# Copies of V and of bias tables in DRAM paced one by one by TensorE, half of V's made earlier, and 12 filler steps instead of 8 ahead of the second attention half

## The chip, the cores and the metric

The kernel runs on one core of one Trainium2 chip. The metric is the device time of one execution in microseconds (us), lower is better; where several executions are measured, their median is taken. The core has a matrix engine (TensorE, PE in the profile), VectorE (DVE), ScalarE (ACT) and GpSimd (POOL), and a queue that issues nearly all transfers in this kernel, SyncE (SP, or SPq for its queue). The engines work through their own instruction streams in order and wait for each other by semaphores.

## The reference

One layer of an encoder on x (1 x 2048 x 1024, float32). After a layer norm with modulation, one input projection (1024 to 9216 columns) feeds two branches: a bidirectional gated linear recurrence (8 heads of 128) and a neighbourhood attention on a grid of 32 rows x 64 columns (16 heads of 64). One output projection, the gated residual and a last layer norm follow. Cut to what bears on the change:

```
def _hgrn2_branch(q_in, i_in, zf_fw, zf_bw, g_in, lb_fw, lb_bw, norm_g):
    ...
    o = direction(zf_fw, lb_fw, False) + direction(zf_bw, lb_bw, True)
    o = _rmsnorm(o.transpose(0, 2, 1, 3), norm_g).reshape(B, S, HG_WIDTH)
    return o.astype(g_in.dtype) * jax.nn.silu(g_in)

def _neighbourhood_attention(q, k, v, rpb):
    """2-D neighbourhood attention. ...
    Each query (r, col) attends to the KR x NA_KC window clamped inside the grid.
```

The attention adds a bias from the table rpb to each score; a query sees 8 rows x 16 columns.

## The kernel before

The sequence is worked on in two halves of 1024 tokens, and the work of TensorE is written out in its final order, a main stream woven with a dense stream of projections. The order of SyncE's, ScalarE's and VectorE's instructions is set by a scheduler with its own estimate of time, except for instructions marked `pinned`, which keep the order of the program among themselves.

The stages are: startup; the first attention half (8 head pairs) up to about 545 us of the trace; the recurrence, 16 units (8 heads by two sequence halves) of `hgrn`, woven with the projections of the unit to come, up to about 1745; the second attention half, 8 head pairs; and the rest of the output projection, up to 2632.

*Weights.* `dma` loads a piece of weights into `wr` (L251, L790), ScalarE copies it to `wh` (L257) and VectorE takes the rest `wl` (L258), so that a float32 product is made of three faster matmuls (L267, L280 for V). Four `wr` buffers go round.

*V.* `vproj` (L280, evacuated as `vt` at L286) writes V of a group of two head pairs to a DRAM tensor `nv_d[p2]` (L288), p2 = 0 to 3, both halves of the sequence. The second attention half reads V column window by column window. `window(p2, j)` (L1360) copies for one of four column offsets j all 32 grid rows, 32 columns each, from `nv_d[p2]` to `nw_d[p2]`, 1 MB from DRAM to DRAM, so that the loads at L978 (`V<-nw`, or `q<-nw` where the buffer's name is that of q) are simple ones. The source rows of the first sequence half are written in the first attention half, those of the second half only near the border.

*The border.* The last unit of the recurrence is woven with `border_dense`: V's projection for p2 = 0, the projections for the first head pair of the second half, V's projection for p2 = 1. Behind dense steps 7, 15, 23 and 31 it calls `window(0, j)`. The unit's own tail (`hgrn_tail`) loads tiles `cl` from DRAM: `cl<-qb` (L666), `cl<-op` (L667), `cl<-sgd` (L668); TensorE multiplies (L671), VectorE adds (L672), and the norm follows: `t` (ScalarE, L331), `rh` (VectorE, L333), sums on TensorE (L339, L340), and a store `yq<-t` (L347). L344 is the product of that norm which reads the `cl` tile for the last time.

*The second attention half.* Before it, K of the first pair is copied by ScalarE into `KA` and `KB` (L970), each on one half of the partitions, and a DMA mirrors it to the other half (L971); Q (L954, L955) and the gate `sg` (L990) are made. TensorE starts with 8 filler steps of V's projection for p2 = 2 and 3 (`vs`; a step is 24 matmuls at L280), then come the scores of the first pair (L1038, L1042). The other filler steps are woven into the first pair. In the pairs u = 0 to 2, `window(u + 1, j)` is called at the task steps 1, 2, 3 and 4.

*Tables.* `expand()` writes the bias tables of the second half in DRAM, as a side stream of the recurrence that is advanced once per group (two groups per unit): first one DMA that fills the parts of `ebot_d` outside the grid with a large negative number (L747, 64 x 24 rows of 256 numbers, all read from one source row; called the fill here), then 24 steps (8 pairs x 3) of three table copies (L744). All are `pinned`. A second side stream, `wo_prepare`, splits the output weights (L414 to L420: `bk`, `wod`). `op`, `qb` and `sgd` (L653 to L659) are the recurrence's own stores.

Of the kernel before, what the change touches and what calls it, by code (L numbers as in the profile page):

```python
# [19 lines left out]
P = 128  # L20
KT = D // P
HALF = 1024
GRP = 512
NHEAD = 8
NPAIR = 8
GW = 64
# [6 lines left out]
KS = (0, 8, 24, 32)  # L33
# [4 lines left out]
def body(ctx: ExitStack, tc: tile.TileContext, t):  # L38
    nc = tc.nc
    dve, act, pool, pe = nc.vector, nc.scalar, nc.gpsimd, nc.tensor  # L40
    dma = nc.sync.dma_start
# [22 lines left out]
    def dram(name, shape, dt=F32):  # L64
        if name in t:
            return t[name]
        return nc.dram_tensor(name, shape, dt, kind="Internal").ap()
# [11 lines left out]
    nv_d = [dram(f"nv{i}", (SEQ, 256)) for i in range(4)]  # L79
    nw_d = [dram(f"nw{i}", (4, SEQ // 2, 256)) for i in range(4)]  # L80
# [49 lines left out]

    def pinned(ins):
        return tc.keep_in_program_order(ins)

    def mod_init():
        mod["c"] = tl("cb", shape=[P, D])
        cs = [cp.tile([P, KT], F32, name=f"cs{i}") for i in range(2)]
        dma(cs[0], t["c"])
        act.activation(cs[1], cs[0], AF.Exp, scale=-1.0)
        sigmoid(cs[1])
        dve.tensor_mul(cs[1], cs[0], cs[1])  # L140
        act.dma_start(c_d.rearrange("(p k) -> p k", k=KT), cs[1])
        act.dma_start(mod["c"], c_d.rearrange("(o n) -> o n", o=1).to_broadcast([P, D]))
        dve.tensor_scalar(adab1, adab[:, 8:16], 1.0, 1.0, op0=ALU.mult, op1=ALU.add)
# [264 lines left out]
    aside = []  # L408
# [13 lines left out]
    def hgrn(u, half, st, tail):  # L422
# [8 lines left out]
        def rates(d, g):  # L431
            col = d * 8 + u
            e = zs[d, g]
            dve.tensor_scalar_min(e, e, ECAP)
            L = tl("g")
            act.activation(L, e, AF.Ln, bias=1.0)
            c = tl("c")
            act.activation(c, e, AF.Ln, scale=lbt[:, col:col + 1], bias=1.0)
            r = tl("g")
            act.activation(r, L, AF.Exp, scale=-1.0, bias=l1m[:, col:col + 1])  # L440
            dve.tensor_tensor(e, e, r, op=ALU.mult)
            for b in range(4):
                lo, hi = b * P, (b + 1) * P
                if d == 0:
                    sl = slice(lo, hi)
                else:
                    sl = slice(hi - 1, lo - 1 if lo else None, -1)
                dve.tensor_tensor_scan(c[:, sl], c[:, sl], L[:, sl], 0.0, op0=ALU.add, op1=ALU.subtract)
            return c, e
# [20 lines left out]
        def turned(src, tag):  # L470
            pk = ps("tr")
            for b in range(4):
                pe.transpose(pk[:, b * P:(b + 1) * P], src[:, b * P:(b + 1) * P], ident)  # L473
            ke = tl(tag)
            act.activation(ke, pk, AF.Copy)
            return ke
# [100 lines left out]
        for g in range(2):  # L577
            v = turned(vts[g], "v")
            next(tail, None)
            cs, ks = {}, {}  # L580
            cs[0], ks[0] = rates(0, g)
            yield 5
            next(tail, None)
            cs[1], ks[1] = rates(1, g)
            de0 = ends(0, g, cs[0], ks[0])
            yield 5
            next(tail, None)
            ke0 = turned(de0, "ke")
            de1 = ends(1, g, cs[1], ks[1])
            kx, qx = diagonal_factors(g, cs, ks)  # L590
            yield 3
            next(tail, None)
            forward_states(g, updates(ke0, v))
            ke1 = turned(de1, "ke")
            yield 3
            next(tail, None)
            pu = updates(ke1, v)
            if g == 0:
                ub = tl("ub")
                act.activation(ub, pu, AF.Copy)  # L600
                ubs[g] = ub
            else:
                ubs[g] = pu
            pb = diagonal(kx, qx)
            lf = [(w, *level_factors(w, g, cs, ks)) for w in (32, 64)]
            yield 6
            next(tail, None)
            pa = ps("pa")
            for w, xk, xq in lf:
                level(w, pa, xk, xq)  # L610
            pm = masked(pa, pb)
            yield 5
            outputs(g, v, pm)
            for z in aside:
                next(z, None)
# [120 lines left out]
    def flat(tab, offset, *dims):  # L736
        return bass.AP(tab.tensor, offset, [list(d) for d in dims])

    def expand():

        def put(dst, row, off, width, tab, jt, nrow, row0, nq, n):
            src = tab[jt, 0, row0, 0, 0:1]
            to = dst[row, off:off + 1]
            pinned(dma(flat(to, to.offset, (width, 16), (16 * width, nq), (1, n * 64)), flat(src, src.offset, (nrow * 64, 16), (64, nq), (1, n * 64))))  # L744

        to, big = ebot_d[0, 0, 0, 0:1], tint[0, 0, 0, 0, 0, 0:1]
        pinned(dma(flat(to, to.offset, (768, 64), (P * 768, NPAIR * 3), (1, 256)), flat(big, big.offset, (0, 64), (0, NPAIR * 3), (1, 256))))  # L747
        for p in range(NPAIR):
            for jt in range(3):
                put(emid_d[p, jt], 0, 0, 960, tint[p], jt, 22, 0, 8, 15)  # L750
                put(ebot_d[p, jt], 0, 256, 768, tedge[p], jt, 15, 0, 4, 8)
                put(ebot_d[p, jt], 64, 0, 768, tint[p], jt, 22, 4, 4, 12)
                yield
# [157 lines left out]
    NLEN = 2 * len(NCOL) * KT * KUS  # L911
    VLEN = 8 * 2.9
# [442 lines left out]
            st = nxt  # L1355
        return r

    def window(p2, j):
        src, to = nv_d[p2][KS[j], 0:1], nw_d[p2][j, 0, 0:1]
        dma(flat(to, to.offset, (32 * 256, 32), (1, 32 * 256)), flat(src, src.offset, (GW * 256, 32), (1, 32 * 256)))  # L1360

    def border_dense(dense):
        yield from vstream(0)
        for i, s in enumerate(dense):
            yield s
            if i % 8 == 7 and i < 32:
                window(0, i // 8)
        yield from vstream(1)

    BTOT = NLEN + 2 * VLEN  # L1370
# [48 lines left out]
    with psum_phase("h", *HPS), phase("h", HB, SMH), tc.manual_schedule(engines={mybir.EngineType.PE}):  # L1419
# [4 lines left out]
        for i in range(16):  # L1424
            half, u = divmod(i, 8)
            if i < 15:
                nxt = hgrn_dense((i + 1) % 8, (i + 1) // 8, i in (6, 7), reload if i == 6 else None)
                tail, st = weave(hgrn(u, half, st, tail), nxt, HTOT, HSUM, lead=20 * KUS if i == 0 else 0.0)
            else:
                raws, dense = natten_stream(0, 1)  # L1430
# [139 lines left out]
    with psum_phase("n1", *NPS), phase("n1", NB1, SM1), tc.manual_schedule(engines={mybir.EngineType.PE}):  # L1570
        natten_init(6, 1)
        st = st0
        for f, *a in ((st.k, 0), (st.k, 1), (st.k, 2), (st.q, 1), (st.table, "mid", 0), (st.table, "mid", 1), (st.table, "mid", 3), (st.v, 0), (st.v, 1), (st.v, 2), (st.v, 3), (st.q, 2), (st.v, 4), (st.gate, 1)):
            f(*a)
        def border_values():
            for i, s in enumerate(vstream(2, 3)):
                yield s
                if i == 13:
                    feed.split(1)

        vs = border_values()
        for _ in range(8):
            next(vs)
        pipe = []
        cts = [(c + u * P) // P for u in range(1, 8) for _ in range(2 if u == 7 else 1) for n, c in NCOL]
        feed = Feed(cts)
        feed.at = 0
        for u in range(8):
            nxt, extra = None, {j + 1: [(window, u + 1, j)] for j in range(4)} if u < 3 else None
            if u < 7:  # L1590
                raws, dense = natten_stream(u + 1, 1, feed, u + 1 == 7)
                total = NLEN
                if u == 0:
                    dense, total = chain(vs, dense), NLEN + VLEN
                nxt = Prep(u + 1, 1, raws)
                if u == 6:
                    extra = {6: [(wo_get, 0, 0)], 7: [(wo_get, 0, 1)], 9: [(wo_get, 0, 2)], 10: [(wo_get, 0, 3), (y_split, 0)], 11: [(wo_get, 0, 4, 5), (y_early, 2)]}
                    for i in (2, 3):
                        extra[i] = [(lambda tt: y_early(tt, alloc=lambda: tl("wr")), i - 2)]
            else:  # L1600
                y_split(1)
                dense, total = out_stream(list(range(NE))), NE * 16 * KUS
                wo_get(0, 6, 7)
                y_early(3)
                extra = {1: [(wo_get, 1, 0, 1)], 2: [(wo_get, 1, 2)], 3: [(wo_get, 1, 3, 4)], 4: [(wo_get, 1, 5)], 5: [(wo_get, 1, 6, 7)]}
            weave(natten_woven(st, nxt, pipe, extra), dense, total, 24)
            st = nxt
        sums(pipe, 2)
        turn(pipe, 2)
        turn(pipe, 1)  # L1610
        sums(pipe, 0)
# [70 lines left out]
```

## Time and profile before

| what | value |
|---|---|
| runs before | 2630.04 us median of 3 (2628.11 to 2630.34) |
| profiled execution | 2633.74 us |
| its span | 2632.0 us, mean granted clock 0.994 |
| matmuls (L267, L280 and all others) | 17328 |
| copies nw<-nv | 16, 1024 KB each |
| table copies emid<-tint, ebot<-tedge, ebot<-tint | 24 each, and the fill |

The profile shows one execution, with times from the start of the span. A wait row reads: engine, waiting tile and line, the releaser, then total us, number of waits, longest. A row of the chain of waits reads: start, duration, what ran or was under way, each step released by the one above; a DMA in it runs from its issue to its landing. A timeline row has start, duration, engine, line, operation, output<-input, shape, and in brackets the idle time of the engine before it with what ended it. A row of windows has the stretch, its length, the busy time with the number of instructions, TensorE's granted clock (1.00 is full speed), the DMA engines' share and GB/s. Lines are those of the kernel before.

### The profile page before, as it was taken

The numbers are of one execution on the slowest core, as the hardware profiler recorded it, in microseconds if no ns is written. First come the engines' busy times: TensorE is split into PE (matmuls) and PEld (weight loads), VectorE is DVE, ScalarE is ACT, GpSimd is POOL, SyncE is SP. The second block draws the span as 40 slices with busy tenths as digits, with TensorE's granted clock in tenths as the row PEclk, the third lists the DMA queues.
The fourth block names the chain that finished last, engine by engine and source line by source line (L and its number), as shares of the span: only waits on it lengthen the run. The fifth ranks groups of instructions, "written<-read, shape, count | busy, mean of one in ns | idle before, by whom it ended". The sixth has DMA issues, their size and how long they took to land.

```text
span 2632.0 us, 45961 instructions
## 1 busy us (share of the span) xinstructions
PE 2570.7 (98%) x17328; PEld 2150.6 (82%) x17328; DVE 1756.1 (67%) x4351; ACT 1417.5 (54%) x2808; POOL 97.9 (4%) x119
## 2 busy tenths in 40 slices
PE   5999999999999999999999999989999999999998
PEld 3888888878888888888888888788888888788887
DVE  6446445478777778877778777546778888658443
ACT  4434445376666666666667666345666666531110
POOL 0000000000000000000000000000000000032221
PEclk9999999999999999999999999999999999999999
DMA  7555454243233337333221222567444445643331
GB/s 261 170 171 156 135 184 138 98 99 135 96 103 114 106 124 261 129 107 98 95 84 57 73 73 81 165 203 255 130 136 135 136 147 181 200 148 128 97 96 56
DMA packets 246061, 352.83 MB, mean 134 GB/s; under 512 B 31575, under 2 KB 121943, under 8 KB 245207
## 3 DMA queue, kind: packets, MB, share of 16 engines
q1 hardware_dynamic: 245551, 349.37, 41.5%
q8 instruction: 136, 2.23, 0.3%
q14 instruction: 86, 0.70, 0.1%
q10 hardware_dynamic: 288, 0.53, 0.1%
HBM read 266.21 MB, written 113.39 MB: 144 GB/s over the span
## 4 chain that ended last, share of the span: by engine, by line
PE 89%; DMA 4%; DVE 4%; ACT 2%; issue 1%; SPq 0%; DVEq 0%; ACTq 0%
PE pj L267 49%; PE pj L280 6%; PE ps L1499 4%; PE ps L1498 4%; PE ps L1500 4%; PE ps L1106 4%; PE ps L1087 3%; PE ps L481 2%; PE ps L1038 2%; PE ps L473 1%; PE ps L1042 1%; PE ps L548 1%; DMA nw<-nv 1%; PE ps L572 1%; PE ps L574 1%; PE ps L520 1%
## 5 line engine op out<-in xcount | busy, mean ns | idle before, releaser
L267 PE MATMUL pj<-h,wh 128*128 128x512 f32 x4016 | 1278.7, 399 | 9.0 <-ACT h L232 5.9
L267 PEld LDWEIGHTS pj<-h,wh 128*128 128x128 f32 x4016 | 731.5, 188 | 165.7 <-issue 13.4
L267 PE MATMUL pj<-h,wl 128*128 128x512 f32 x2008 | 787.3, 392 | 0.0
L267 PEld LDWEIGHTS pj<-h,wl 128*128 128x128 f32 x2008 | 377.4, 188 | 82.5
L1060 ACT ACTIVATE pbuf<-pbuf,mx 128x480 f32<-128x480 f32 (+2 forms) x224 | 143.0, 639 | 143.1 <-DVE mx L1055 142.2
L280 PE MATMUL pj<-wh,h 128*128 128x256 f32 x1024 | 193.2, 287 | 0.9 <-ACT wh L826 0.7
L1055 DVE CUSTOM_DVE_ANT_1 pbuf<-ps,bias 128x480 f32<-128x480 f32 (+2 forms) x224 | 125.8, 590 | 101.1 <-PE ps L1042 85.8
L258 DVE TENSOR_TENSOR wl<-wr,wh 128x512 fp32r<-128x512 f32 x192 | 131.5, 685 | 53.8 <-ACT wh L257 53.0
L280 PEld LDWEIGHTS pj<-wh,h 128*128 128x128 f32 x1024 | 162.3, 192 | 4.7 <-issue 1.9
L257 ACT ACTIVATE wh<-wr 128x512 fp32r<-128x512 f32 x192 | 120.0, 625 | 68.3 <-PE pj L267 55.9
L280 PE MATMUL pj<-wl,h 128*128 128x256 f32 x512 | 145.2, 284 | 0.4 <-DVE wl L827 0.4
L1093 ACT ACTIVATE pt<-ps 128x512 f32<-128x512 f32 (+1 forms) x128 | 68.9, 538 | 85.9 <-PE ps L1087 84.2
L1091 DVE COPY pt<-ps 128x512 f32<-128x512 f32 (+1 forms) x128 | 79.0, 619 | 49.6 <-PE ps L1087 48.9
L774 ACT ACTIVATE e<-pj 128x512 f32<-128x512 f32 x100 | 59.1, 592 | 89.0 <-PE pj L267 83.5
L1471 ACT ACTIVATE yh<-yr 128x512 fp32r<-128x512 f32 x52 | 32.7, 629 | 134.6 <-PE ps L1499 115.7
L1087 PE MATMUL ps<-ident,pbuf 128*128 128x128 f32 x776 | 103.3, 273 | 0.0
L1087 PEld LDWEIGHTS ps<-ident,pbuf 128*128 128x128 f32 x776 | 90.8, 141 | 13.6 <-issue 0.2
L1554 DVE TENSOR_TENSOR vt<-ps,gt 128x512 f32<-128x512 f32 x24 | 16.5, 692 | 128.1 <-PE ps L1500 128.1
L827 DVE TENSOR_TENSOR wl<-wr,wh 128x512 fp32r<-128x512 f32 x68 | 46.8, 690 | 80.8 <-ACT wh L826 76.6
L280 PEld LDWEIGHTS pj<-wl,h 128*128 128x128 f32 x512 | 98.5, 192 | 1.3 <-DVE wl L827 0.6
L1065 DVE TENSOR_SCALAR pbuf<-pbuf,mx 128x480 f32<-128x480 f32 (+2 forms) x224 | 96.0, 437 | 5.4
L1106 PE MATMUL ps<-pt,V 128*64 128x128 f32 x1408 | 96.7, 277 | 0.8 <-DMA V<-nv 0.8
(278 smaller groups left out, 4694.3 us busy)
## 6 DMA issues: line engine op xcount, KB each, us to landing
wr<-in_w_in SPq DMA_DIRECT2D x276, 256.0 KB
nw<-nv SPq DMA_DIRECT2D x16, 1024.0 KB
yr<-yq SPq DMA_DIRECT2D x60, 256.0 KB
emid<-tint SPq DMA_DIRECT2D x24, 480.0 KB
bias<-emid SPq DMA_DIRECT2D x24, 480.0 KB
V<-nw SPq DMA_DIRECT2D x40, 256.0 KB
bias<-ebot SPq DMA_DIRECT2D x24, 384.0 KB
x<-in_x SPq DMA_DIRECT2D x32, 256.0 KB
```

The costliest lines, as they stand in the source:

```text
L257: act.activation(hi, raw, AF.Copy)
L258: dve.tensor_tensor(lo, raw, hi, op=ALU.subtract)
L267: pe.matmul(pz, a, b, start=(k == 0 and n == 0), stop=(k == KT - 1 and n == 2))
L280: pe.matmul(pzs[tp][:, i * 256:(i + 1) * 256], a, b, start=(k == 0 and n == 0 and i == 0), stop=(k == KT - 1 and n == 2), skip_group_check ...
L1055: return dve.tensor_tensor_reduce(s[:, 0:nk].rearrange("p (r c) -> p r c", c=32), sc[:, 0:nk].rearrange("p (r c) -> p r c", c=32), bt[:, 0 ...
L1060: act.activation(s[:, 0:nk], s[:, 0:nk], AF.Exp, scale=-1.0, bias=mx[:, 0:1], accum_out=mx[:, 1:2])
L1065: dve.tensor_scalar(s[:, 0:nk], s[:, 0:nk], mx[:, 2:3], 1.0, op0=ALU.mult, op1=ALU.mult)
L1087: pe.transpose(ptp[:, c * P:(c + 1) * P], s[:, c * P:(c + 1) * P], ident)
L1106: pe.matmul(self.po[R][hs_, j * P:(j + 1) * P], self.st.V[c0 + c][:, j * P + hh * 64:j * P + hh * 64 + 64], pts[hh][:, c * P:(c + 1) * P], ...
L1498: pe.matmul(pz, yh[:, kk], wh, start=first, stop=False)
L1499: pe.matmul(pz, yh[:, kk], wl, start=False, stop=False)
L1500: pe.matmul(pz, yl[:, kk], wh, start=False, stop=last)
```

## The change

- `paced(ins)` is new: it makes a DMA wait for the TensorE instruction that was emitted last before it in the program. The fill, the table copies and the V copies use it; the first two were `pinned`, the V copies had neither.
- `window` has a third argument, the sequence half, and copies 16 grid rows, 512 KB, so that there are 32 copies.
- The copies of half 0 go into `expand()`: four steps, one for each j, ahead of the tables of pairs 0, 2, 4 and 6. `expand()` begins with 8 empty steps and is advanced once more per group, in the middle of it. It had 24 steps with copies and now has 8 empty ones and 40 with copies; both end with unit 11.
- The copies of half 1 stay where the whole ones were, further apart: for p2 = 0 behind dense steps 5, 17, 29 and 41 of the border, for the others at task steps 3, 5, 7 and 9 of the pairs u = 0 to 2.
- 12 filler steps instead of 8 come ahead of the first scores of the second half; four are left for the first pair, whose `total` is smaller accordingly.

The number of matmuls and their operands stay. Lines in the changed kernel are higher: by 5 up to the new `next(aside[1], None)`, by 16 in the second attention half; `window` is at L747, the fill at L759, the table copies at L756.

```
+    def paced(ins):
+        mm = next(i for i in reversed(nc.cur_bb.bb.instructions) if i.engine == mybir.EngineType.PE)
+        tc.add_manual_dep(ins.ins, mm.name, mybir.DependencyInfo(mybir.DependencyClass.Sync, mybir.DependencyReason.DATA), reason="paced")
+        return ins
...
             yield 3
+            next(aside[1], None)
             next(tail, None)
             pu = updates(ke1, v)
...
+    def window(p2, j, half):
+        src, to = nv_d[p2][half * HALF + KS[j], 0:1], nw_d[p2][j, half * (HALF // 2), 0:1]
+        paced(dma(flat(to, to.offset, (32 * 256, 16), (1, 32 * 256)), flat(src, src.offset, (GW * 256, 16), (1, 32 * 256))))
+
     def expand():
+        for _ in range(8):
+            yield
...
         for p in range(NPAIR):
+            if p % 2 == 0:
+                for j in range(4):
+                    window(p // 2, j, 0)
+                    yield
...
         for i, s in enumerate(dense):
             yield s
-            if i % 8 == 7 and i < 32:
-                window(0, i // 8)
+            if i % 12 == 5:
+                window(0, i // 12, 1)
...
         vs = border_values()
-        for _ in range(8):
+        for _ in range(12):
             next(vs)
...
-            nxt, extra = None, {j + 1: [(window, u + 1, j)] for j in range(4)} if u < 3 else None
+            nxt, extra = None, {2 * j + 3: [(window, u + 1, j, 1)] for j in range(4)} if u < 3 else None
...
                 if u == 0:
-                    dense, total = chain(vs, dense), NLEN + VLEN
+                    dense, total = chain(vs, dense), NLEN + VLEN / 2
```

The order of SyncE's instructions in the last unit of the recurrence, at the loads `cl` of its tail, was:

```order
L1360 DMA nw<-nv 32x8192 x4
L666 DMA cl_18170<-qb 128x512
L347 DMA yq<-t_18029 128x512
L251 DMA wr_18526<-in_w_v 128x512
L978 DMA q_19443<-nw 128x4x128
L978 DMA q_19445<-nw 128x4x128
L667 DMA cl_18171<-op 128x512
L251 DMA wr_18532<-in_w_v 128x512
```

At the same place it is now:

```order
L747 DMA nw<-nv 16x8192
L352 DMA yq<-t_18045 128x512
L672 DMA cl_18186<-qb 128x512
L256 DMA wr_18542<-in_w_v 128x512
L673 DMA cl_18187<-op 128x512
L747 DMA nw<-nv 16x8192
L256 DMA wr_18548<-in_w_v 128x512
L352 DMA yq<-t_18183 128x512
```

One half copy instead of four whole ones stands ahead of `cl<-qb`; the two loads from `nw` that stood ahead of `cl<-op` have gone behind the fourth half copy, 14 to 17 rows on.

ScalarE's order ahead of the first scores of the second half was (`vt` is the last evacuation of V's projection in the border, `wh` a weight split of a filler step, `KA` and `KB` the keys):

```order
L286 ACTIVATE vt_19050<-pj_18950 128x512
L257 ACTIVATE wh_19181<-wr_19179 128x512
L257 ACTIVATE wh_19187<-wr_19185 128x512
L970 ACTIVATE KA_3600_18870<-bk_17580 64x512
L970 ACTIVATE KB_3601_18871<-bk_17580 64x512
L970 ACTIVATE KA_3600_18870<-bk_17582 64x256
```

At the same place it is now:

```order
L291 ACTIVATE vt_19066<-pj_18966 128x512
L986 ACTIVATE KA_3600_18886<-bk_17596 64x512
L986 ACTIVATE KB_3601_18887<-bk_17596 64x512
L986 ACTIVATE KA_3600_18886<-bk_17598 64x256
L986 ACTIVATE KB_3601_18887<-bk_17598 64x256
L986 ACTIVATE KA_3600_18886<-e_18300 64x256
L986 ACTIVATE KB_3601_18887<-e_18300 64x256
L970 ACTIVATE Q_18907<-bk_17594 64x512
L971 ACTIVATE Q_18908<-bk_17594 64x512
L970 ACTIVATE Q_18927<-e_18155 64x512
L971 ACTIVATE Q_18928<-e_18155 64x512
L1006 ACTIVATE sg_18935<-bk_17600 128x512
```

The two weight splits have moved from ahead of the keys to behind the gate `sg`. On TensorE 96 matmuls of the filler steps have moved ahead of the first scores.

SyncE's order around the fill was, at the start of the recurrence:

```order
L251 DMA wr_5719<-in_w_in 128x512
L251 DMA wr_5725<-in_w_in 128x512
L414 DMA bk_5749<-in_w_out 128x512
L747 DMA ebot<-tint 64x24x256
L744 DMA emid<-tint 16x8x960
L744 DMA ebot<-tedge 16x4x512
L744 DMA ebot<-tint 16x4x768
L251 DMA wr_5871<-in_w_in 128x512
```

The fill is now in the third unit of the recurrence:

```order
L256 DMA wr_7526<-in_w_in 128x512
L759 DMA ebot<-tint 64x24x256
L747 DMA nw<-nv 16x8192
L256 DMA wr_7681<-in_w_in 128x512
L256 DMA wr_7687<-in_w_in 128x512
L425 DMA wod<-bk_7270 128x512
L747 DMA nw<-nv 16x8192
```

A half copy of V stands behind it in place of three table copies, and weight loads follow both.

More of the change, by code (lines that the diff above doesn't have):

```diff
@@ L743, in put @@
             to = dst[row, off:off + 1]
-            pinned(dma(flat(to, to.offset, (width, 16), (16 * width, nq), (1, n * 64)), flat(src, src.offset, (nrow * 64, 16), (64, nq), (1, n * 64))))
+            paced(dma(flat(to, to.offset, (width, 16), (16 * width, nq), (1, n * 64)), flat(src, src.offset, (nrow * 64, 16), (64, nq), (1, n * 64))))
         to, big = ebot_d[0, 0, 0, 0:1], tint[0, 0, 0, 0, 0, 0:1]
-        pinned(dma(flat(to, to.offset, (768, 64), (P * 768, NPAIR * 3), (1, 256)), flat(big, big.offset, (0, 64), (0, NPAIR * 3), (1, 256))))
+        paced(dma(flat(to, to.offset, (768, 64), (P * 768, NPAIR * 3), (1, 256)), flat(big, big.offset, (0, 64), (0, NPAIR * 3), (1, 256))))
         for p in range(NPAIR):
+            if p % 2 == 0:
+                for j in range(4):
+                    window(p // 2, j, 0)
+                    yield
             for jt in range(3):
@@ L1356, in first_half @@
         return r
-    def window(p2, j):
-        src, to = nv_d[p2][KS[j], 0:1], nw_d[p2][j, 0, 0:1]
-        dma(flat(to, to.offset, (32 * 256, 32), (1, 32 * 256)), flat(src, src.offset, (GW * 256, 32), (1, 32 * 256)))
     def border_dense(dense):
```

## The prediction

> **What bounds the kernel now.** I read the page first, then the waits of TensorE, then the chain of waits around its two late holes, and last the queue and ScalarE rows that feed these holes.
>
> ```profile
> span 2632.0 us, 45961 instructions
> PE 2570.7 (98%) x17328; PEld 2150.6 (82%) x17328; DVE 1756.1 (67%) x4351; ACT 1417.5 (54%) x2808; POOL 97.9 (4%) x119
> ```
>
> TensorE is busy for 98% of the span, and the change neither adds nor drops a matmul. So it can win only time in which TensorE stands, or runs at a lower clock: 2632.0 - 2570.7 = 61.3 us of standing in all. The waits of TensorE (engine, line, releaser: total us, times, longest) say who ended them:
>
> ```profile
> PE ps L1038 <- DMA KA<-KA: 8.3, 1, 8.3
> ...
> PE ps L339 <- DVE rh L333: 3.2, 2, 2.9
> ...
> PE ps L481 <- ACT ke L475: 1.6, 1, 1.6
> ...
> PE ps L572 <- ACT c L438: 0.9, 1, 0.9
> ...
> PE ps L671 <- DMA cl<-qb: 0.6, 1, 0.6
> ```
>
> The chain of waits from 1655 to 1780 us (start, duration, what) holds three of them, in two places.
>
> ```profile
> 1661.73 13.77 DMA nw<-nv
> ...
> 1675.57 0.37 SPq L978
> ...
> 1676.54 5.96 DMA cl<-op
> ...
> 1682.59 0.70 DVE cl L672
> ...
> 1684.45 0.80 PE ps L339
> ...
> 1723.33 2.41 DMA yq<-t
> ...
> 1728.27 2.88 PE pj L280 x24
> ...
> 1746.45 15.72 DMA nw<-nv
> ...
> 1765.73 5.41 DMA KA<-KA
> ...
> 1771.28 1.94 PE ps L1038 x4
> ```
>
> **Place A (1676 to 1691 us).** The last of four 1 MB V copies lands 13.77 us after its issue, at 1675.50. SyncE has stood at the load q<-nw, which reads these copies, until 1675.57, and cl<-op, queued behind, goes out only at 1676.54. From there it runs through VectorE (1682.59) and ScalarE to L339 at 1684.45: a hole of 2.90 us, after one of 0.64 us at L671.
>
> **Place B (1763 to 1778 us).** The second burst ends with 15.72 us to landing, the mirror copies KA<-KA come behind it, and the first scores, L1038, start at 1771.28 after 8.30 us of standing. The queue's timeline (start, us over all of the row's issues, their count) gives both bursts and the mirrors:
>
> ```profile
> 1659.90 2.61 SPq L1360 DMA_DIRECT2D nw<-nv  x4
> ...
> 1744.66 2.53 SPq L1360 DMA_DIRECT2D nw<-nv  x4
> ...
> 1762.68 0.50 SPq L971 DMA_DIRECT2D KA<-KA  x1
> ```
>
> Both holes also cost clock, as the windows of TensorE show (busy, granted clock):
>
> ```profile
> 1684.00:1688.00 4.00, 3.54 (x13) 0.52 0.44 154
> 1688.00:1692.00 4.00, 4.00 (x14) 0.63 0.41 132
> 1770.00:1774.00 4.00, 2.72 (x8) 0.50 0.92 270
> 1774.00:1778.00 4.00, 4.00 (x25) 0.71 1.05 309
> ```
>
> After A the ungranted clock is 0.48 x 4.00 = 1.92 us, less half of the 0.45 us in which TensorE still stood, and 0.37 x 4.00 = 1.48 us: 3.2 us. After B it is half of 2.72 and 0.29 x 4.00: 2.5 us. So A costs 0.64 + 2.90 + 3.2 = 6.7 us and B 8.30 + 2.5 = 10.8 us; together 17.5 us.
>
> **The change, part by part.** *V copies cut in halves.* Sixteen issues of 1 MB become 32 of 512 KB. Four copies took 1675.50 - 1659.90 = 15.6 us, so one half costs the queue at most 15.6 / 8 = 2 us. In SyncE's order cl<-op now comes before the second half copy, and the loads q<-nw have gone behind the fourth. What cl<-op then waits for is the tile that it fills, which VectorE gives back here:
>
> ```profile
> 1672.61 0.69 DVE L344 TENSOR_TENSOR t<-t,cl 128x512 f32<-128x512 f32 x1 [2.15 <-ACT t L343]
> ```
>
> So it can go out at 1673.3 and lands at 1675.7 if it takes 2.41 us as yq<-t of the same 256 KB did, at 1679.3 if it takes the old 5.96. VectorE also needs L671:
>
> ```profile
> 1676.59 1.10 PE L671 MATMUL ps<-cl,Sb 128*128 128x512 f32 x2 [0.64 <-DMA cl<-qb]
> ```
>
> Without its 0.64 us L671 ends at 1677.1. From L672 to L339 the chain takes 1684.45 - 1682.59 = 1.86 us, so L339 may start at 1679.0 at best and 1681.2 at worst; TensorE gets there at 1684.45 - 2.90 - 0.64 = 1680.9. The hole becomes 0 to 0.3 us, and I take 0, since one half copy lies ahead now and not four whole ones. For cl<-qb one half (2 us) and 2.41 us after 1665.6 is 1670, 6 us early. Next late is the ScalarE and VectorE work between two uses, which L339's other wait puts at 3.2 - 2.9 = 0.3 us.
>
> *No second burst, and 12 filler steps ahead.* The burst at 1744.66 is gone; the halves for the next pair lie two steps apart inside the first pair. Four filler steps move ahead of the first scores, 24 matmuls of L280 in 2.88 us each: L1038 is reached 11.5 us later, at 1762.98 + 11.5 = 1774.5, at no cost, as the same steps leave the first pair. ScalarE's order changes as well. Its rows before:
>
> ```profile
> 1750.55 1.31 ACT L286 ACTIVATE vt<-pj 128x512 f32<-128x512 f32 x2 [3.21 <-PE pj L280]
> 1754.38 0.63 ACT L257 ACTIVATE wh<-wr 128x512 fp32r<-128x512 f32 x1 [2.51 <-PE pj L280]
> 1757.26 0.63 ACT L257 ACTIVATE wh<-wr 128x512 fp32r<-128x512 f32 x1 [2.25 <-PE pj L280]
> 1757.79 0.62 ACT L970 ACTIVATE KA<-bk 64x512 fp32r<-64x512 f32 x1
> ...
> 1763.47 0.63 ACT L990 ACTIVATE sg<-bk 128x512 f32<-128x512 f32 x1
> ```
>
> Two weight splits stood ahead of the key copies and waited 2.51 and 2.25 us for TensorE. Now the key copies come right behind vt (1751.86), 1757.79 - 1751.86 = 5.9 us earlier; the mirrors follow, and with 2.41 to 5.41 us to land the last is there by about 1760 to 1763, against 1774.5. B is covered by over 11 us. The price is at the ninth filler step: its weight split stands behind the key copies and sg, so it starts at about 1763.47 - 5.9 + 0.6 = 1758.2 instead of 1754.38, and VectorE still has to take the rest from it; TensorE comes at 1762.98. That is some 3 us of margin, and if it went, the cost would be a hole of 1 to 2 us.
>
> *Half of V's copies and all table copies in the recurrence, each waiting for TensorE.* These are 16 halves, 72 table copies and the fill, one DMA of 64 x 24 rows of 1 KB. Behind each on SyncE stand weight loads. SyncE's own waits say how it is paced already (total, times, longest):
>
> ```profile
> SPq L251 <- DVE wl L258: 390.0, 86, 13.8
> ```
>
> At the weight loads SyncE stands 390 us anyway, since a load waits until its buffer has been split for TensorE. A copy that waits for the TensorE instruction emitted just before it is released at about the same progress, so I cost the waits at nothing; the buffers loaded ahead hide them, and the bound if they don't is the first rival. The fill is the one copy with a visible price (queue timeline, chain of waits, ScalarE's wait, window):
>
> ```profile
> 544.85 0.63 SPq L747 DMA_DIRECT2D ebot<-tint  x1
> ```
> ```profile
> 555.24 21.77 DMA wr<-in_w_in
> ```
> ```profile
> ACT wh L257 <- DMA wr<-in_w_in: 1.9, 1, 1.9
> ```
> ```profile
> 560.00:565.00 5.00, 3.92 (x20) 2.91 (x18) 4.08 (x11) 2.80 (x6) 0.00 (x0) 1.00 0.81 75
> ```
>
> A weight load behind fill and three table copies landed at 577.0, ScalarE waited 1.9 us for it, and TensorE 0.9 us at L572. Alone the fill takes between 1.57 MB at 75 GB/s = 21 us and 577.0 - 544.85 = 32 us; I take 23, since three table copies lay in the longer figure. It now stands between weight loads of the third unit:
>
> ```profile
> 700.63 11.90 SPq L251 DMA_DIRECT2D wr<-in_w_in  x3
> ```
> ```profile
> 733.66 0.63 ACT L257 ACTIVATE wh<-wr 128x512 fp32r<-128x512 f32 x1 [0.96 <-PE pj L267]
> ```
>
> Issued soon after 700.63, near 704, it is through at 727, a half copy at 729, the weights behind at 731.4: 2.3 us before ScalarE wants them at 733.66. The old 0.9 us goes, and a new one of 0 to 0.9 us may come: -0.4 us. For 88 copies at new places I add one hole of the size that table copies have caused, 0.9 us (bounds: 0, and two of 1.6 us, as at L481).
>
> [...]
>
> On the size of a hole that costs clock: the 1.6 us hole at L481 lies in the window 560 to 565, whose clock is 1.00, and the 2.90 us one at A brought 0.52. [...] So a rest of up to 1.6 us is priced at its length, and one near 3 us at twice that.
>
> **The sum.** -6.7 - 10.8 - 0.4 + 0.9 = -17.0 us. The profiled execution took 2633.74 us, 1.7 more than its span; it becomes 2616.7. The median of the runs is 3.7 us lower, and the same difference gives 2630.04 - 17.0 = 2613.0 us.
>
> **The rivals.** (1) *Waiting copies hold the weight loads, slower.* SyncE serves in order, so a copy released late delays every load behind it, and TensorE then waits for weights. One such place costs what A did, 2.90 + 3.2 = 6.1 us. To lose over 5.3 us net it takes 17.0 + 5.3 = 22.3 us, four such places: 2637 us with four at 24.4 us. There are 40 steps with copies in the recurrence. Against it stands that, next to the 1.9 us above, the recurrence and the border have one wait of an engine for a weight load:
>
> ```profile
> DVE wl L258 <- DMA wr<-in_w_v: 0.6, 1, 0.6
> ```
>
> Chance 0.04.
> (2) *The fill starves the third unit.* At 32 us instead of 23, weights are 7 us late against a margin of 2.3; TensorE stands 2 to 4 us and loses as much in clock: +4 to +8 us, 2617 to 2621. Chance 0.10. (3) *Only one place is closed.* At A the chain behind cl<-op stays late, or at B the ninth filler step takes the mirrors' place: only B gives 2619.2, only A 2623.3. For it: margins of 2 and 3 us. Chance 0.12. (4) *It does not do what it says*: the scheduled order keeps the waits, or half copies spread everywhere cost in small holes what the two gave. Within 5.3 us of 2630; chance 0.06. The forecast keeps 0.68.
>
> **How the numbers follow.** About 0.2%, 5.3 us, is what a measurement here can tell from no change. The forecast's own bounds are -18.4 (no new hole, 0.9 won) and -14.7 (3.2 us of new holes): 2611.6 to 2615.3; the low end goes 1.9 us further by the spread of the runs before, and a little for small waits behind the bursts: 2609. Rival 2 reaches 2621, with the better half of rival 3; that leaves out some 0.16. Faster: 0.68 + 0.10 + 0.12 = 0.90; same 0.06; slower 0.04.
>
> **What would show it.** TensorE's waits no longer name KA<-KA at L1038, nor over 0.5 us at L339 and L671; clock 1.00 in both windows; cl<-op issued at once behind L344; no 1024 KB issue left. The fill near 704 with the next weights landing by 732 and no ScalarE wait at L257 shows its step right. The prediction is wrong if TensorE waits for wh or wl in the recurrence, or at the ninth filler step, or if a hole over 2 us stays at L339.

## The result, and the profile after

The changed kernel took 2613.1 us (median of 4, 2611.63 to 2614.25), the kernel before 2630.19 (median of 4, 2628.11 to 2633.5). The ratio is 0.9934, 95% interval 0.9916 to 0.9951: 17.1 us less, which was forecast as 17.0. The profiled execution took 2614.25 us, 19.5 less than that of before. One of the five executions of e9 below took 2839.28 us at a granted clock of 0.85; it counts in the median given for e9, but not in its ratio. The page after:

```profile
span 2612.5 us, 46055 instructions
PE 2565.1 (98%) x17328; PEld 2147.1 (82%) x17328; DVE 1756.1 (67%) x4351; ACT 1417.6 (54%) x2808; POOL 98.2 (4%) x119
```

All matmuls are still there; TensorE stands for 47.4 us in place of 61.3 and is busy 5.6 us less, which goes with a mean granted clock of 0.998 in place of 0.994: the windows at 0.50 to 0.71 behind A and B are at 1.00 now. Its waits from 540 to 1745 us, the stretch that holds the recurrence and place A (engine, line, releaser: total us, times, longest):

```profile
PE ps L486 <- ACT ke L480: 1.6, 1, 1.6
PE ps L577 <- ACT gt L384: 1.3, 1, 1.3
PE ps L486 <- DVE Sf L497: 0.9, 1, 0.9
PE ps L345 <- DVE rl L340: 0.5, 2, 0.3
PE ps L344 <- DVE rh L338: 0.3, 1, 0.3
PE pj L285 <- ACT e L790: 0.3, 1, 0.3
```

Gone are the 2.9 us at L339 (now L344), the 0.6 us at L671 and the 0.9 us at L572 behind `c`. The chain of waits shows TensorE without a break at A (L344 at 1678.75) and up to the first scores (L1054, before L1038), at B:

```profile
1675.29 3.46 PE pj L272 x15
1678.75 0.24 PE ps L344
1678.98 0.23 PE ps L345
...
1736.74 28.76 PE pj L285 x236
1765.50 0.89 PE ps L1054 x4
```

TensorE's windows at both places (length, busy, granted clock, DMA share, GB/s) have the full clock:

```profile
1676.00:1680.00 4.00, 4.00 (x23) 1.00 0.71 244
1680.00:1684.00 4.00, 4.00 (x25) 1.00 0.26 88
...
1762.00:1766.00 4.00, 4.00 (x33) 1.00 0.74 256
1766.00:1770.00 4.00, 4.00 (x31) 1.00 0.40 135
```

And the queue, with `cl<-op` ahead of the second half copy at A, and the first and last mirror copy at B, which were issued at 1762.68 to 1767.70 before:

```profile
1671.31 0.32 SPq L673 DMA_DIRECT2D cl<-op  x1
1671.98 0.49 SPq L747 DMA_DIRECT2D nw<-nv  x1
...
1743.43 0.50 SPq L987 DMA_DIRECT2D KA<-KA  x1
...
1746.62 0.55 SPq L987 DMA_DIRECT2D KB<-KB  x1
```

Where the 19.5 us of the two profiled executions come from is read by following single matmuls through both traces:

| matmul, line before | before | after | gained up to here | in this stretch |
|---|---|---|---|---|
| L481 behind its 1.6 us hole | 565.50 | 564.86 | 0.64 | 0.64 startup, where the code is the same |
| L572 behind its 1.3 us hole | 610.82 | 608.87 | 1.95 | 1.31 the fill's old place |
| L340 in the recurrence's last third | 1457.08 | 1455.12 | 1.96 | 0.01 |
| L280 behind place A | 1710.77 | 1701.59 | 9.18 | 7.22 place A |
| L1500 at the end of the second half | 2246.62 | 2227.13 | 19.49 | 10.31 place B |

The stretch that holds place A, from the third mark to the fourth, takes 253.7 us before, 252.1 in the experiment e1 below and 246.4 to 246.5 in the other ten kernels. From the fourth mark to the end of the span it is 921.2 us before, 921.4 in e8, 913.3 in e1 and 910.4 to 911.0 in the other nine.

### The profile page after: what moved, and what is told of

It is laid out like the page before. It is cut to its first block, busy times and chain, and to the rows that moved or that the text cites. A ratio compares the mean times of both kernels' runs of the same rounds, so it can differ in the third digit from the quotient of the medians.

```text
span 2612.5 us, 46055 instructions
## 1 busy us (share of the span) xinstructions
PE 2565.1 (98%) x17328; PEld 2147.1 (82%) x17328; DVE 1756.1 (67%) x4351; ACT 1417.6 (54%) x2808; POOL 98.2 (4%) x119
## 4 chain that ended last, share of the span: by engine, by line
PE 92%; DVE 3%; DMA 3%; ACT 2%; issue 1%; SPq 0%; DVEq 0%; ACTq 0%
PE pj L272 51%; PE pj L285 6%; PE ps L1510 4%; PE ps L1512 4%; PE ps L1511 4%; PE ps L1122 4%; PE ps L1103 3%; PE ps L486 2%; PE ps L1054 2%; PE ps L478 2%; PE ps L553 1%; PE ps L1058 1%; PE ps L577 1%; PE ps L579 1%; PE ps L525 1%; PE ps L654 1%
```

## The experiments

The theory at this point: the gain is the two places A and B, each a copy burst in front of a transfer that TensorE waits for. The rivals: the filler steps, the earlier copies or the waits for TensorE each carry part of it. In all, ten kernels ran; times are medians, ratios are to the kernel before on the same chip.

| run | us | ratio (95%) | holes that matter |
|---|---|---|---|
| e1 before, 12 filler steps | 2623.49 | 0.9979 (0.9971, 0.9988) | A stays; 2.18 at the ninth step |
| e2 changed, 8 filler steps | 2611.75 | 0.9940 (0.9928, 0.9953) | none |
| e3 changed, not paced | 2623.05 | 0.9979 (0.9970, 0.9988) | 5.39 at 676 |
| e4 changed, no early half | 2612.41 | 0.9940 (0.9928, 0.9953) | none |
| e5 changed, fill from other rows | 2612.69 | 0.9933 (0.9919, 0.9946) | none |
| e6 e3, fill from other rows | 2615.29 | 0.9945 (0.9932, 0.9957) | 0.66 to 2.00, four of them |
| e7 e3, fill in 24 pieces | 2615.80 | 0.9945 (0.9932, 0.9957) | 0.24 to 2.20, four of them |
| e8 before, A's copies spread and paced | 2624.25 | 0.9977 (0.9967, 0.9986) | 7.95 at B |
| e9 before, all V copies spread and paced | 2615.56 | 0.9947 (0.9934, 0.9961) | 0.95 at 580 |
| e10 e9, fill from other rows | 2613.89 | 0.9940 (0.9927, 0.9954) | none over 1 beyond those of all kernels |

**e1: the filler steps alone.**

```
-        for _ in range(8):
+        for _ in range(12):
             next(vs)
...
-                    dense, total = chain(vs, dense), NLEN + VLEN
+                    dense, total = chain(vs, dense), NLEN + VLEN / 2
```

> The kernel before with one part of the change alone: 12 filler steps instead of 8 ahead of the second attention half. The V copies stay whole, unpaced and in their two bursts, and ScalarE still splits the two filler weights ahead of the keys. Theory (the four filler steps alone cover place B): the mirrors land at 1771.2 as before, TensorE reaches the first scores 11.5 us later, at 1774.5, so the 8.3 us hole and its 2.5 us of clock go; place A keeps its 2.9 us hole and 3.2 us of clock. Time 2630.2 - 10.8 = 2619.4 us. Rival (the burst itself is what costs at B; something else behind it takes the mirrors' place): a hole of several us stays at the scores or at the ninth filler step, 2625 to 2630 us.

Measured: 5.5 us less than before, not 10.8, and between the ranges of theory and rival. The wait for the mirrors went, as the theory has it, and a new one came, as the rival has it. ScalarE and then TensorE at the ninth step:

```profile
1749.22 0.63 ACT L257 ACTIVATE wh<-wr 128x512 fp32r<-128x512 f32 x1 [2.50 <-PE pj L280]
1752.10 0.63 ACT L257 ACTIVATE wh<-wr 128x512 fp32r<-128x512 f32 x1 [2.25 <-PE pj L280]
...
1759.37 1.07 ACT L286 ACTIVATE vt<-pj 128x512 f32<-128x512 f32 x2
```
```profile
1760.00 0.39 PE L280 MATMUL pj<-wh,h 128*128 128x256 f32 x1 [2.18 <-ACT vt L286]
```

In this trace ScalarE went through its rows in the order they were given in. The two weight splits, which waited 2.50 and 2.25 us for TensorE, stand ahead of the keys, and the evacuation `vt` of TensorE's results behind the keys: TensorE waited 2.18 us for ScalarE, which had waited for TensorE. 10.8 - 2.2 = 8.6 us would be left of the gain. The two traces roughly agree with this: behind place A e1 takes 913.3 us in place of 921.2, which is 7.9 less. The medians show only 5.5, and their interval reaches 7.6. The traces do not explain this difference; by whole executions they are 13.1 us apart, as the traced one of before is slower than its median and that of e1 is the fastest of its eleven.

**e2: the change without the additional filler steps.**

```
-        for _ in range(12):
+        for _ in range(8):
             next(vs)
...
-                    dense, total = chain(vs, dense), NLEN + VLEN / 2
+                    dense, total = chain(vs, dense), NLEN + VLEN
```

> The changed kernel with 8 filler steps instead of 12; all else of the change stays. In the changed kernel's trace the last mirror copy was issued at 1746.62, and the nearest transfers land 2.0 to 5 us after their issue; without the four steps TensorE reaches the first scores at 1765.5 - 11.5 = 1754.0. Theory (without the burst the mirrors are early anyway, so the four steps are a second cover of the same wait): no hole at the scores, 2613 us, within 1.5 us of the changed kernel. Rival (the four steps are what closes B): a hole of up to 8 us and a drop of the clock come back, 2619 to 2624 us.

Measured: the time of the changed kernel. The chain has no wait at the first scores, which now come 15 us earlier:

```profile
1734.97 15.34 PE pj L285 x126
1750.31 0.89 PE ps L1054 x4
```

Here the mirrors were issued by 1743.19 and on the way before TensorE asked for them. So without the burst the four steps are not needed.

**e4: no early half.** The recurrence makes no copies of V; each later place makes both halves.

```
                 for j in range(4):
-                    window(p // 2, j, 0)
                     yield
...
             if i % 12 == 5:
+                window(0, i // 12, 0)
                 window(0, i // 12, 1)
...
-            nxt, extra = None, {2 * j + 3: [(window, u + 1, j, 1)] for j in range(4)} if u < 3 else None
+            nxt, extra = None, {2 * j + 3: [(window, u + 1, j, 0), (window, u + 1, j, 1)] for j in range(4)} if u < 3 else None
```

> The changed kernel without V's early copies: the recurrence makes none (its steps stay empty there), and each later place makes two half copies in place of one, still paced. So the border again moves 4 MB. Theory (spreading the copies over the border is enough; moving half of them ahead buys nothing): two halves, 4 us, ahead of cl<-qb, which TensorE wants 10 us after its issue; no hole over 0.5 us at A, 2613 to 2614 us. Rival (it is the volume in the border that holds up the cl loads): a hole of 1 to 3 us at L339 or L671, with up to 3 us of clock, 2615 to 2619 us.

Measured: 2612.41 us, no hole at A or B. 1 MB at a place is as good as 512 KB; what was moved ahead bought nothing.

**e3: the waits taken out.** `paced` only keeps the program order of the copies.

```
     def paced(ins):
-        mm = next(i for i in reversed(nc.cur_bb.bb.instructions) if i.engine == mybir.EngineType.PE)
-        tc.add_manual_dep(ins.ins, mm.name, mybir.DependencyInfo(mybir.DependencyClass.Sync, mybir.DependencyReason.DATA), reason="paced")
-        return ins
+        return pinned(ins)
```

> The changed kernel with all its DRAM copies kept in program order among themselves, as the table copies were before, and none waiting for TensorE. In the order of SyncE three half copies of V then stand in a row ahead of cl<-qb in the border, the loads from nw stay behind the fourth, and the fill comes one unit earlier. Theory (what counts at A is what stands ahead of the cl loads; the order does it, the wait only keeps that order): three halves are 1.5 MB, about 6 us, cl<-op still goes out ahead of the loads from nw, so at A a hole of 0 to 1 us is left: 2613 to 2616 us. Rival (without the wait the copies bunch again and the holes come back): 3.5 us and 3.2 us of clock at A, 2620 us, or more if the copies bunch in the recurrence too.

Measured: A and B are closed without any wait, as the theory has it, yet the time is 2623.05, outside its range. The loss lies elsewhere, in a hole at 676 us that no other kernel has:

```profile
681.82 1.22 PE L270 MATMUL pj<-h,wh 128*128 128x512 f32 x2 [5.39 <-issue]
```
```profile
676.00:680.00 4.00, 0.42 (x2) 0.00 (x0) 3.93 (x11) 2.27 (x5) 0.00 (x0) 1.00 0.53 202
680.00:684.00 4.00, 2.19 (x5) 1.80 (x6) 2.88 (x8) 0.00 (x0) 0.00 (x0) 0.64 0.63 233
684.00:688.00 4.00, 4.00 (x16) 3.52 (x16) 1.12 (x2) 1.69 (x3) 0.00 (x0) 0.51 0.00 2
```

"issue" means that TensorE waited for nothing the profile shows; no operand is named as late. The fill was issued at 654.03 in this kernel and took 26.3 us, to 680.4. The DMA view by queue, first for 654 to 678 us (all transfers of the stretch are on the kernel's own queue) and then for 678 to 684 (the instruction queue moves two packets):

```profile
q1 hardware_dynamic: 1640, 1.90, 54.2%
```
```profile
q1 hardware_dynamic: 664, 1.51, 67.2%
q8 instruction: 2, 0.03, 1.9%
```

So no packet of the instruction queue moved from 654 to 678 us while the fill ran, and two did in the 6 us in which it ended: one between 678 and 680, before the fill landed, and one between 682 and 684. In the changed kernel, too, no packet of this queue moved from 700 to 724 us, under its fill (a second instruction queue, q14, moved one between 700 and 701, before the fill was issued at 701.69), and TensorE had no hole there. A second theory, the author's guess at this point: the fill holds TensorE's instruction fetch as it holds the weight loads (22.5 and 20.9 us to land behind it in the changed kernel). e5, e6, e7 and e10 test this and what makes the fill slow.

**e5 and e6: the fill reads other rows.** One edit, in the changed kernel and in e3:

```
-        paced(dma(flat(to, to.offset, (768, 64), (P * 768, NPAIR * 3), (1, 256)), flat(big, big.offset, (0, 64), (0, NPAIR * 3), (1, 256))))
+        paced(dma(flat(to, to.offset, (768, 64), (P * 768, NPAIR * 3), (1, 256)), flat(big, big.offset, (1408, 64), (13 * 1408, NPAIR * 3), (1, 256))))
```

> The changed kernel with one edit: the fill of 1536 pieces of 1 KB reads some 360 different source rows in DRAM, all holding the same number, in place of one row 1536 times. Order and sizes stay. In the changed kernel the fill took 26.6 us from issue to landing and two weight loads behind it 22.5 and 20.9. Theory (the fill is slow because all of its pieces read one row): it lands in 5 to 10 us, the weight loads behind it in under 8; the time stays within 1.5 us of the changed kernel's 2613, since TensorE had no hole there. Rival (pieces of 1 KB between DRAM and DRAM are slow as such): landing stays at 24 to 28 us.

> The kernel with the halves not paced (2623.05 us, with a new hole of 5.39 us at 676 in which TensorE waited for nothing that the profile shows, while the fill was under way), with one edit: the fill reads some 360 different rows in place of one. SyncE's order is the same row for row. Theory (the slow fill holds all transfers, TensorE's instruction fetch among them; the wait for TensorE is not what the change gains by): the hole at 676 and its clock loss of about 3 us go, 2613 to 2615.5 us. Rival A (the fill is slow by its piece size, so nothing changes): hole and time stay, 2623. Rival B (the hole is not the fill's): the fill is faster but the hole stays.

Measured in e5: the fill landed 7.0 us after its issue (26.6 in the changed kernel), the two weight loads behind it after 3.3 and 3.4 us (22.5 and 20.9), and the time stayed. The windows of the changed kernel and of e5 while the fill runs:

```profile
713.00:718.00 5.00, 5.00 (x32) 4.41 (x31) 4.93 (x15) 3.50 (x7) 0.00 (x0) 1.00 0.94 66
```
```profile
705.00:710.00 5.00, 5.00 (x23) 3.94 (x21) 3.88 (x8) 3.78 (x6) 0.00 (x0) 1.00 1.09 377
```

The DMA engines are as busy (0.94 and 1.09), at 66 GB/s with one source row and at 377 with some 360, for pieces of the same 1 KB (in e5 the stretch also holds part of the half copy behind the fill). So neither the piece size nor DRAM to DRAM is what was slow in this fill, but the one row.

Measured in e6: the hole at 676 is gone, with SyncE's order the same row for row, and in the stretch 654 to 678 the instruction queue now moves its two packets:

```profile
q8 instruction: 2, 0.03, 0.6%
```

Rivals A and B fall: the slow fill made the hole. That it did so by way of the instruction fetch is what the queue rows suggest, not what they show: no row says which engine a packet is for, and the fetch alone was not varied. 2615.29 us is at the upper end of what the theory gave. The trace of e6 has small holes of 0.66, 0.94, 0.80 and 2.00 us in the recurrence where that of the changed kernel has one of 0.9; by their times alone e5 and e6 are not told apart (0.9919 to 0.9946 and 0.9932 to 0.9957).

**e7: the fill in pieces**, in e3, at each of the 24 steps with table copies.

```
-        paced(dma(flat(to, to.offset, (768, 64), (P * 768, NPAIR * 3), (1, 256)), flat(big, big.offset, (0, 64), (0, NPAIR * 3), (1, 256))))
...
             for jt in range(3):
+                row = ebot_d[p, jt, 0, 0:1]
+                paced(dma(flat(row, row.offset, (768, 64), (1, 256)), flat(big, big.offset, (0, 64), (1, 256))))
                 put(emid_d[p, jt], 0, 0, 960, tint[p], jt, 22, 0, 8, 15)
```

> The kernel with the halves not paced, with the fill cut into 24 pieces of 64 KB, each issued with the table copies of its own step; each still reads one source row 64 times. Theory (what costs is one transfer that holds the queue for 26 us): a piece takes a twenty-fourth, about 1.1 us; no hole over 1.6 us in the recurrence, 2613 to 2616 us. Rival (unpaced copies of V are what stalls TensorE in the recurrence): a hole of some us stays near the early copies, 2618 to 2623.

Measured: 2615.8 us; no hole at 676, and pieces that land in 2.5 to 6.3 us. The time is the theory's, but its bound on the holes failed: one of 2.20 us at 1056, where it allowed 1.6. e6, whose fill is fast, has one of 2.00 us at the same place, and the changed kernel 0.9; so the pieces are not what makes it, and in that the rival has a part.

**e8 and e9: only the spreading.** e8 makes the four whole copies of the border where the changed kernel makes its halves, paced; e9 does so with all 16 copies. (`paced` is added, and `window` takes it as a third argument.)

```
-            if i % 8 == 7 and i < 32:
-                window(0, i // 8)
+            if i % 12 == 5:
+                window(0, i // 12, paced)
```

In e9 this is added:

```
-            nxt, extra = None, {j + 1: [(window, u + 1, j)] for j in range(4)} if u < 3 else None
+            nxt, extra = None, {2 * j + 3: [(window, u + 1, j, paced)] for j in range(4)} if u < 3 else None
```

> The kernel before with one part of the change alone: the four 1 MB copies of the border's first burst are made behind dense steps 5, 17, 29 and 41 and each waits for TensorE. Whole copies, no early half, second burst, 8 filler steps and fill as before. In SyncE's order one copy then stands ahead of cl<-qb and the loads from nw have gone behind the fourth. Theory (A is worth 6.7 us and is closed by spreading alone): no hole over 0.5 us at L339 or L671, clock 1.00 there, B as before: 2629.0 - 6.7 = 2622.3 us; the profile of before lies above its median, so 2622 to 2625. Rival (whole copies are too long, a half is needed): 1 to 3 us of hole at A stay, 2625 to 2628.

> The kernel before with the V copies spread and waiting for TensorE, and nothing else of the change: 16 whole copies of 1 MB, for the first group behind dense steps 5, 17, 29 and 41 of the border, for the others at task steps 3, 5, 7 and 9 of the first three pairs. No halves, no early copies, 8 filler steps, table copies and fill as before. In ScalarE's order the keys then come right behind V's last evacuation. Theory (spreading closes both places, the rest of the change is not needed): no hole over 0.5 us at A and none at the first scores, clock 1.00 in both; the small holes of the kernel before in the recurrence stay (0.9 at 580 us). 2613.1 + 1 = 2614 us, 2612 to 2616. Rival (each part of the change carries some of the gain): a hole of 1 us or more at A or at the first scores, 2616 to 2620.

Measured in e8: 2624.25 us, in the theory's range; A has no hole, and B, whose burst stays, is as before:

```profile
1763.07 0.74 PE L1043 MATMUL ps<-KA,Q 128*128 128x480 f32 x1 [7.95 <-DMA KA<-KA]
```

Measured in e9: 2615.56 us, in the theory's range of 2612 to 2616, with neither A nor B. Its ratio, 0.9934 to 0.9961, overlaps with that of the whole change. ScalarE's order has changed with the second burst: in e8, which keeps it, two weight splits still stand between `vt` and the keys; in e9 the keys come right behind `vt`, as in the changed kernel.

**e10: e9 with the fill from other rows.**

> The same kernel with the fill, at its old place at the start of the recurrence, reading some 360 different source rows in place of one. Theory (the 0.9 us hole near 580 us comes from the weight load behind the slow fill): that hole goes and ScalarE's wait of 1.9 us for the weight load with it; 0 to 1 us less than the kernel it starts from, 2611 to 2615. Rival (three table copies behind the fill hold the load as much): hole and wait stay.

Measured: 2613.89 us. In e9 the old waits are there (ScalarE's, then TensorE's):

```profile
ACT wh L262 <- DMA wr<-in_w_in: 2.1, 1, 2.1
```
```profile
PE ps L577 <- ACT c L443: 1.0, 1, 1.0
```

In e10 both are gone; the fill lands after 9.3 us instead of 28.2, and the weight load behind it after 2.6 instead of 22.0. The same three table copies stand behind the fill, so the rival falls. Neither wait comes in every execution, though: in e1, with the slow fill at the old place, ScalarE waited 0.6 us and TensorE not at all. No version here is clearly faster than the changed kernel: e2, e4, e5 and e10 are all within its interval.

## Why the prediction was right, point by point

**Place A**, 6.7 us forecast, 7.22 us between the two traces: the step held. `cl<-op` went out at 1671.31, at once ahead of the second half copy. With the 1.96 us gained up to there that is the 1673.3 of the prediction. Neither L339 nor L671 waits. e3, e4, e8 and e9 close A in four other ways, and all have this in common: at most three half copies ahead of `cl<-qb`, and the loads from `nw` behind `cl<-op`. In the trace of before, `cl<-op` stood behind the load that waits for the burst, 3.2 us past 1673.3, and `cl<-qb`, issued behind the burst, made L671 wait. All four runs make the row ahead of `cl<-qb` shorter and move those loads away; which of the two counts for more is not shown.

**Place B**, 10.8 us forecast, 10.31 us between the traces: the size held, but one cover more was named than it takes. e9 differs from e8 only in the copies that come after the border, those of the second burst first among them, and B goes with that burst. How the burst holds the mirrors is in SyncE's own waits from 1735 to 1775 us of before, which the prediction did not read:

```profile
SPq L790 <- DMA nw<-nv: 3.7, 1, 3.7
```

A weight load stood until the burst had landed, and the first mirror went out right behind it, at 1762.68. The other way is ScalarE's order, in which the keys came later with the burst. The runs change both together, so their shares stay open. The prediction put two things in the way of the wait, the missing burst and the 11.5 us of filler steps. e2 shows that the first is enough; e1 that the second alone closes the wait for the mirrors and opens one of 2.18 us behind ScalarE. The doubt about the ninth filler step was thus sound, but for e1 and not for the changed kernel.

**The fill**, -0.4 us forecast, 1.31 us gained at its old place and no loss at its new one: mis-sized. The gain is partly luck of the trace. From the first mark of the table to the second, the kernels with the slow fill at its old place take 45.3 (before), 45.7 (e8) and 45.6 us (e9), but e1, with the same fill there, takes 44.0, as all kernels without it do. At its new place the fill took 26.6 us, not the 23 taken. Its weights landed at 730.5 (708.00 + 22.5), and ScalarE wanted them at 731.70, so that the margin was 1.2 us and not 2.3. ScalarE's row, and the fill's issue:

```profile
701.69 0.63 SPq L759 DMA_DIRECT2D ebot<-tint  x1
```
```profile
731.70 0.63 ACT L262 ACTIVATE wh<-wr 128x512 fp32r<-128x512 f32 x1 [0.95 <-PE pj L272]
```

The prediction had the weight loads as the only ones behind the fill. By the queue rows instruction packets may have been behind it as well: the changed kernel had no hole there, while e3, with the fill one unit earlier, lost 5.39 us and, by its windows of 0.64 and 0.51, some 3 us of clock. That is the size that rival 2 gave, in another kernel and by a way that it did not name; the prediction did not weigh it for the changed kernel either.

**The allowance of 0.9 us for new holes** was not needed on balance: the third mark of the table shows 0.01 us lost or won between 609 and 1455, where a hole of 0.90 us at 1054 has come in place of one of 0.79 at 986.

**The waits for TensorE at no cost**: held. There is no wait of TensorE for `wh` or `wl` in the recurrence, so rival 1 did not come about. Without the waits the traces of e3, e6 and e7 have 1.8, 4.4 and 4.1 us of small holes in the recurrence (the hole at 676 aside), against 1.1 us in the changed kernel. That the waits are what spares them is likely, but these are single executions.

**The sum.** From trace to trace it is 19.5 us where 17.0 was forecast: 0.5 more at A, 0.5 less at B, 0.9 more at the fill, 0.9 of allowance not used, and 0.64 in the startup, which the change does not touch. That the medians differ by 17.1, almost the forecast, is owed in part to the profiled execution of before, which is 3.6 us slower than its median, while that of the changed kernel is only 1.2 us slower. The single terms are to be compared with the traces, and there they are good to 1 us each.

## What to carry to other kernels

Look for what stands in an in-order queue behind a load that waits for a large transfer: the load and the transfer may have time, and the small one behind them may not, as at A, where `cl<-op` went out at 1676.54 behind a load that had stood until 1675.57 us. Spreading the large transfers, with a wait for TensorE, gave the whole gain here as far as the intervals of some 3 us to either side can tell. Cutting them in halves, moving half of them ahead and giving TensorE more work in front showed no effect once they were spread (2613.1 us with all of it, 2611.75 in e2, 2612.41 in e4, 2615.56 in e9). A fill from one row looks harmless by its 1.5 MB, and the weight loads behind it landed only after 20.9 and 22.5 us.

## What the runs showed of the hardware

- 1536 pieces of 1 KB read from one source row of 1 KB in DRAM took 26.3 (e3) to 28.3 us (before); from some 360 source rows 7.0 (e5) to 9.3 us (e10).
- TensorE stood in e3 for 5.39 us without a wait that the profile shows, behind such a fill, under which the instruction queue had moved nothing for 24 us; with the fill from other rows (e6) that queue moved two packets in the same stretch, and TensorE did not stand there. By which way the fill held TensorE is not shown.
- Holes of 1.58 (L481, before) and 2.18 us (e1) left the clock at 1.00; holes of 2.00 (e6), 2.20 (e7), 2.62 (e1, place A) and 2.90 us (before, place A) were followed by windows at 0.57, 0.71, 0.50 and 0.52. So in these traces the length alone does not decide near 2 us. TensorE's windows behind the hole of 1.58 us in before (the window that the prediction read, 560 to 565, ends before the hole does), then behind the one of 2.00 us in e6, over the end of the one of 2.20 us in e7 and what follows it, and from the middle of the one of 2.18 us in e1:

```profile
566.00:569.00 3.00, 3.00 (x19) 1.00 0.94 113
```
```profile
1058.00:1062.00 4.00, 4.00 (x75) 0.57 0.30 104
```
```profile
1058.00:1062.00 4.00, 3.34 (x74) 0.71 0.42 150
```
```profile
1759.00:1761.00 2.00, 1.00 (x8) 1.00 1.06 330
1761.00:1763.00 2.00, 2.00 (x19) 1.00 0.76 170
```

The prediction's rule, up to 1.6 us at its length and near 3 us at twice that, holds at its two ends (1.58 us, and 2.90 us with 3.2 us of clock); between them the hole of 2.18 us in e1 cost its length, and the one of 2.00 us in e6, with 0.43 x 4.00 = 1.7 us of ungranted clock behind it, nearly twice that.
